# A hybrid attention trunk on one core: residual copies placed inside the paired stage, the last pair summed on chip, compression weights three pieces ahead, a shorter last norm

## The chip, the core and the metric

The kernel runs on one core of a Trainium2 chip. It computes on TensorE (PE, matmuls), VectorE (DVE), ScalarE (ACT) and GpSimd (POOL). DMA transfers are issued by the queues of SyncE (SP), POOL and, at the very start, ACT. The metric is the device time of one execution in microseconds.

## What is computed

A row of 256 tokens of width 4096 passes one layer: an RMS norm, one input projection to two mixers, a gate on each, one output projection, the residual, and a last RMS norm.

```python
h = _rmsnorm(x, norm_g[l])
proj = h @ w_in[l]
(q_a, k_a, v_a, z_a, q_b, kc, vc, ksl, vsl, kwn, vwn, z_b, g_b) = jnp.split(proj, _split_points(), axis=-1)
o_a = _dilated_mixture(...)                     # 16 heads, three strided windows
o_b = _nsa(..., kc, vc, ...)                    # 16 heads; compressed, selected and window keys
y_a = _rmsnorm(o_a, out_g_a[l]) * jax.nn.silu(z_a)
y_b = _rmsnorm(o_b, out_g_b[l]) * jax.nn.silu(z_b)
x = x + jnp.concatenate([y_a, y_b], -1) @ w_out[l]
...
return _rmsnorm(x, final_g)

# in _nsa, for the keys kc and the values vc:
def _compress(t, pe, w1, w2):                   # 15 overlapping blocks of 32 tokens
    flat = blocks(t + pe).reshape(B, n_c, G, CMP_BLOCK * hd)
    return jax.nn.gelu(flat @ w1) @ w2          # w1 is 4096 x 256, w2 256 x 128
```

All data are float32. Each product of float32 operands is done as three matmuls of operands split into a rounded high part and a remainder (`mm3`, lines 98 to 100). The high parts are written by ACT (line 105), the remainders by DVE (line 106).

## The kernel before

Weights are read from memory in chunks of 512 columns. The kernel has five stages.

1. **Start.** A stream of three single chunks. `stage_unit` loads a weight piece of 1 MB (tile `w`, line 249 to 254; three buffers), `load_xT` a piece of x transposed (tile `xp`). ACT scales and splits x (`xh`, line 108) and the weights (`wh`, line 105); DVE writes the remainders `xl` and `wl`.
2. **Paired input stage.** `run_pairs` computes nine pairs of chunks with a Strassen-like scheme: 16 steps a pair, nine of them with seven products, seven plain. Weights are loaded three steps ahead (`bw`, lines 424 and 425, on SP). The products gather in eight PSUM banks. At a pair's last product step of each kind, `put_sums` has ACT copy each bank to a tile `parts` (line 453), and POOL adds it to up to four outputs in memory with accumulating DMAs (`accum_op=add`, line 459; the first of a pair are plain stores, line 457). The ninth pair gives `sel` and `za0`.
3. **Middle stage.** A stream of eight chunks (seven gate chunks, then the first output chunk), beside which the attention work is woven in as tasks. The first tasks are the two `compress` calls (keys, then values): each reads w1 in four pieces of 1 MB (`load_w1`, line 820, SP; pool `o` with four buffers, of which the block tile `bhl` takes one), splits each piece in halves (`w1hl`) and multiplies them into `ph` (lines 872 and 873). The first two pieces are asked for ahead; piece i + 2 is asked for when piece i has been split. Each piece of the stream is called a unit; it too is split in halves.
4. **Paired output stage.** `run_pairs` again, for three pairs, with the residual added: the outputs `r1` to `r4` start as copies of columns of x (line 1326), on which `put_sums` accumulates. The last pair's sums stay on chip (`keep_first`, `keep_rest`).
5. **Last stage.** Two half chunks. ACT squares every part of the result into columns of `ssr` (`square_r`, line 1126). `finish` then sums these, takes the root on POOL (line 115), scales the rows on DVE and ACT and stores them (line 1198), first for tokens 0 to 127, then for the rest.

The paired stages stand in the order in which they are written (`manual_schedule`); in the other stages the scheduler of the language moves instructions that do not depend on what stands ahead of them. Each engine and each queue then works through its own list in order.

Of the kernel before, what the change touches and what calls it, by code (L numbers as in the profile page):

```python
# [18 lines left out]
P = 128  # L19
SEQ = 256  # L20
NT = SEQ // P
DM = 4096
# [61 lines left out]
def hybrid_trunk(ctx: ExitStack, tc: tile.TileContext, a: dict):  # L84
# [309 lines left out]

    def run_pairs(w_src, dcs, lhs_of, sops, begin, places, names, out=False, later=None):

# [76 lines left out]
        def keep_first(ps):  # L473
            t = kept["c11"] = part()
            nc.scalar.activation(t, ps["p1"], AF.Copy)
            for x, y, bank in (("c12", "c11", "p6"), ("c21", "c12", "p7"), ("c22", "c21", "p5")):
                t = kept[x] = part()
                nc.vector.tensor_add(t, kept[y], ps[bank])
            nc.vector.tensor_add(kept["c12"], kept["c12"], ps["p5"])
            for x in kept:  # L480
                nc.vector.tensor_add(kept[x], kept[x], resid[x])
# [22 lines left out]
        for n, (d, i) in enumerate(steps):  # L504
# [11 lines left out]
            if FAST[i]:  # L516
                s = lambda j: (sops[i][:, 0, j], sops[i][:, 1, j])
                e = not any(FAST[k] for _, k in steps[n + 1 : n - n % NKP + NKP])
                raws, sums = -B22, 3
                for bank, lhs, b in (  # L520
                    ("p1", block(i, 0, 0), raws + B11), ("p7", s(2), sums + T3), ("p5", s(0), sums + T1),
                    ("p6", s(1), sums + T2), ("p3", s(3), raws + B22), ("p2", block(i, 0, 1), raws + B21),
                    ("p4", block(i, 1, 1), sums + T4),
                ):
                    product(bank, lhs, b, e and bank in ("p1", "p5", "p6", "p7"))
                if e and out and d == len(dcs) - 1:
                    keep_first(ps)
                elif e:
                    put_sums(d, ps, ("p1", "p7", "p5", "p6"))
            else:  # L530
                e = n % NKP == NKP - 1
                for bank, row, cols in (("p3", 0, (B12, B22)), ("p2", 0, (B11, B21)), ("p4", 1, (B11, B21)), ("e", 1, (B12, B22))):
                    for col, b in enumerate(cols):
                        product(bank, block(i, row, col), b, e and col == 1)
                if e and d == len(dcs) - 1:
                    return lambda: keep_rest(ps) if out else put_sums(d, ps, ("p3", "p2", "p4", "e"))
                if e:
                    put_sums(d, ps, ("p3", "p2", "p4", "e"))
            split_on(n)
            if n == 2 and later:  # L540
                later()

# [286 lines left out]
    def compress(t, which):  # L829
# [26 lines left out]
        for grp in range(9):  # L856
            if grp < 8:
# [5 lines left out]
                if grp % 2 == 1:  # L863
                    load_w1(4 * which + grp // 2 + 2)
                if grp == 4 and which == 0:
# [258 lines left out]
    def square_r(pool, r, m, i):  # L1124
        junk = room[pool].tile([P, r.shape[-1]], F32, name="junk", tag="junk", bufs=1 if i == 0 else 2)
        nc.scalar.activation(junk, r, AF.Square, accum_out=ssr[:, m, i : i + 1])

# [36 lines left out]
    def out_chunk(i):  # L1164
# [3 lines left out]
        def done(ps, only=None):  # L1168
            xr, gf = res["in", i], gf_at(i)
            for m in range(NT) if only is None else [only]:  # L1170
                r = res_at(i, m)
                nc.vector.tensor_add(r, ps[m][:, : OUT_AT[i][1]], xr[:, m])
                square_r("zq", r, m, i)
                if only is None:
                    nc.vector.tensor_mul(r, r, gf)
            if only is not None:
                finish(only, gf)
        return before, done

    def finish(m, gf):  # L1180
        s = room["work"].tile([P, 1], F32, name="sr")
        nc.vector.reduce_sum(s, ssr[:, m], axis=AX.X)
        r = cst.tile([P, 1], F32, name=f"rout{m}")
        rsqrt_mean(r, s, DM)
        for i in range(8):
# [9 lines left out]
            else:  # L1195
                nc.vector.tensor_scalar_mul(t, t, r)
            if i % 2:
                nc.sync.dma_start(a["out"][m * P : (m + 1) * P, (i - 1) * CW : (i + 1) * CW],
                                  res[q, m][:, at - CW : at + CW])

# [62 lines left out]
    ordered.enter_context(tc.manual_schedule())  # L1263
    rest = run_pairs(a["w_in"], dcs, x_lhs, sops, begin_pairs, IN_PLACES, IN_BANKS)
    inner.close()
# [11 lines left out]
    def begin_rest():  # L1277
        rest()
        psum.close()
# [19 lines left out]

    hooks[0, 3] = load_first  # L1300
    hooks[0, 10] = attentions
    z_chunks = [("a", 12, i) for i in range(1, 4)] + [("b", 22, i) for i in range(4)]
# [13 lines left out]
    def before_out():  # L1316
# [7 lines left out]

        for c in range(1, 5):
            nc.gpsimd.dma_start(scratch(f"r{c}"), a["x"][:, c * CW : (c + 1) * CW].rearrange("(m p) c -> p m c", p=P))

    first_out = []
# [21 lines left out]
    ordered.enter_context(tc.manual_schedule())  # L1350
    rest = run_pairs(a["w_out"], dcs, y_lhs, y_sops, begin_out, OUT_PLACES, OUT_BANKS, out=True, later=store_first)
    inner.close()
# [76 lines left out]
```

## Time and profile before

| | us |
|---|---|
| median of three runs (lowest, highest) | 1654.27 (1653.38, 1655.62) |
| profiled execution, time | 1653.73 |
| profiled execution, span | 1651.8 |
| TensorE busy | 1615.9 |
| VectorE busy | 1377.4 |
| ScalarE busy | 999.4 |
| POOL busy | 153.6 |
| mean granted TensorE clock | 0.993 of full |

The span runs from the first to the last instruction; the time has a little around it. Matmuls overlap in the records, so a busy TensorE is not one at its peak; where it stands still is what counts. A row of a timeline gives start, duration, engine, line, operation, output tile <- input tiles, and in brackets how long the engine stood idle before it and what ended that. In rows of the chain of waits the two numbers are start and duration. The weights of `compress`, w1 and w2, read `w<-in_cmp_k_w` in the profile, since numbers at the end of a name are left out.

### The profile page before, as it was taken

To read this page: it belongs to the slowest core of one execution; us is meant where nothing else is said; L and a number is where in the kernel's file an instruction comes from. 1 tells how busy PE (TensorE), PEld (TensorE's weight loads), DVE (VectorE), ACT (ScalarE), POOL (GpSimd) and SP (SyncE) were. 2 spreads that over 40 slices of the span, in tenths; PEclk is the share of its full clock that TensorE was granted. 3 is DMA by queue.
4 is the path that set the end of the run, shared out by engine and by line. 5 is a ranking of instruction groups with operands and counts; after the bars stand their busy time and mean duration, and the time that the engine had idled before them with its cause. 6 is when DMAs were issued, how large, how long until landed. Compare 5 with 4: busy or idle time off the path is not lost.

```text
span 1651.8 us, 20933 instructions
## 1 busy us (share of the span) xinstructions
PE 1615.9 (98%) x7743; PEld 1330.4 (81%) x7743; DVE 1377.4 (83%) x1668; ACT 999.4 (61%) x1255; POOL 153.6 (9%) x207
## 2 busy tenths in 40 slices
PE   8999999999999999999998999999999999999997
PEld 5998778888888888888876777788878877788886
DVE  6769898988899898989856788888877769898884
ACT  6755656565656565656554566766667646656553
POOL 0000111110202020202020000000000000112110
PEclk9999999999999999999998999999999999999999
DMA  9776798888888887979798555633455456798974
GB/s 359 267 244 222 209 276 253 262 250 258 244 259 254 249 268 241 279 237 276 236 326 303 190 172 179 227 138 141 135 179 185 166 196 216 220 282 240 289 289 169
DMA packets 105862, 387.76 MB, mean 235 GB/s; under 512 B 12640, under 2 KB 13280, under 8 KB 94368
## 3 DMA queue, kind: packets, MB, share of 16 engines
q1 hardware_dynamic: 81504, 332.42, 57.3%
q0 software_dynamic: 23824, 52.97, 14.6%
q8 instruction: 60, 0.98, 0.2%
q10 hardware_dynamic: 432, 1.05, 0.2%
q14 instruction: 42, 0.34, 0.1%
HBM read 334.69 MB, written 53.79 MB: 235 GB/s over the span
## 4 chain that ended last, share of the span: by engine, by line
PE 81%; DVE 8%; DMA 5%; issue 3%; ACT 3%; SPq 0%; ACTq 0%; POOLq 0%; POOL 0%; DVEq 0%
PE p L99 15%; PE p L100 15%; PE p L98 15%; PE acc L99 8%; PE acc L100 8%; PE acc L98 8%; DMA w<-in_w_in 2%; PE e L100 2%; PE e L99 2%; PE e L98 2%; DVE bf L439 2%; DVE bt L432 1%; DVE bf L438 1%; DMA w<-in_cmp_k_w 1%; PE pt L1051 1%
## 5 line engine op out<-in xcount | busy, mean ns | idle before, releaser
L106 DVE TENSOR_TENSOR wl<-w,wh 128x1024 fp32r<-128x1024 f32 (+2 forms) x178 | 207.7, 1171 | 90.8 <-ACT wh L105 89.9
L105 ACT ACTIVATE wh<-w 128x1024 fp32r<-128x1024 f32 (+2 forms) x178 | 180.3, 1017 | 111.5 <-PE acc L100 92.4
L98 PE MATMUL acc<-wh,xh 128*128 128x512 f32 (+2 forms) x640 | 244.3, 382 | 3.3 <-ACT wh L105 3.2
L439 DVE TENSOR_TENSOR bf<-bt,bf 128x2048 fp32r<-128x2048 f32 x108 | 246.6, 2283 | 0.0
L99 PE MATMUL acc<-wl,xh 128*128 128x512 f32 (+2 forms) x640 | 241.7, 378 | 2.8 <-DVE wl L106 2.8
L100 PE MATMUL acc<-wh,xl 128*128 128x512 f32 (+2 forms) x640 | 241.3, 377 | 0.0
L434 ACT ACTIVATE bf<-bt 128x1024 fp32r<-128x1024 f32 x108 | 114.6, 1061 | 185.6 <-DVE bt L432 185.3
L106 DVE TENSOR_TENSOR bp<-bw,bp 128x2048 fp32r<-128x2048 f32 x72 | 164.7, 2287 | 72.5 <-ACT bp L105 72.4
L431 ACT ACTIVATE bf<-bw 128x1536 fp32r<-128x1536 f32 x108 | 160.5, 1486 | 65.9 <-DMA bw<-in_w_in 42.6
L105 ACT ACTIVATE bp<-bw 128x2048 fp32r<-128x2048 f32 x72 | 137.7, 1912 | 92.3 <-PE e L100 73.8
L438 DVE TENSOR_TENSOR bf<-bw,bf 128x1536 fp32r<-128x1536 f32 x108 | 189.0, 1750 | 0.0
L437 ACT ACTIVATE bf<-bt 128x1024 fp32r<-128x1024 f32 x108 | 114.8, 1063 | 42.8 <-DVE bt L436 40.2
L432 DVE TENSOR_TENSOR bt<-bw 128x1024 f32<-128x1024 f32 x108 | 131.8, 1221 | 10.0 <-DMA bw<-in_w_in 5.5
L98 PEld LDWEIGHTS acc<-wh,xh 128*128 128x128 f32 x640 | 121.3, 190 | 22.2 <-ACT wh L105 5.4
L99 PEld LDWEIGHTS acc<-wl,xh 128*128 128x128 f32 x640 | 121.4, 190 | 22.0 <-DVE wl L106 5.8
L100 PEld LDWEIGHTS acc<-wh,xl 128*128 128x128 f32 x640 | 121.1, 189 | 19.0
L99 PE MATMUL p<-bf,sum 128*128 128x512 f32 x324 | 127.0, 392 | 1.4 <-DVE bf L439 1.2
L99 PE MATMUL p<-bp,xh 128*128 128x512 f32 x324 | 126.2, 389 | 0.9 <-DVE bp L106 0.9
L98 PE MATMUL p<-bf,sum 128*128 128x512 f32 x324 | 126.3, 390 | 0.0
L100 PE MATMUL p<-bf,sum 128*128 128x512 f32 x324 | 126.2, 390 | 0.0
L100 PE MATMUL p<-bp,xl 128*128 128x512 f32 x324 | 126.0, 389 | 0.0
L98 PE MATMUL p<-bp,xh 128*128 128x512 f32 x324 | 126.0, 389 | 0.0
(325 smaller groups left out, 3413.0 us busy)
## 6 DMA issues: line engine op xcount, KB each, us to landing
bw<-in_w_in SPq DMA_DIRECT2D x288, 512.0 KB, 6.3
w<-in_w_in SPq DMA_DIRECT2D x60, 1024.0 KB, 5.0
bw<-in_w_out SPq DMA_DIRECT2D x96, 512.0 KB, 5.1
w<-in_w_out SPq DMA_DIRECT2D x16, 1024.0 KB, 5.1
scr_q<-parts POOLq DMA_DIRECT2D x30, 256.0 KB, 7.9
scr_k<-parts POOLq DMA_DIRECT2D x30, 256.0 KB, 7.9
scr_v<-parts POOLq DMA_DIRECT2D x30, 256.0 KB, 7.8
scr_qb<-parts POOLq DMA_DIRECT2D x30, 256.0 KB, 7.9
```

The lines of the kernel that those rows point to most:

```text
L98: nc.tensor.matmul(out, lh, rh, start=start, stop=False)
L99: nc.tensor.matmul(out, lh, rl, start=False, stop=False)
L100: nc.tensor.matmul(out, ll, rh, start=False, stop=stop)
L105: nc.scalar.activation(h, src, AF.Copy)
L106: nc.vector.tensor_sub(l, src, h.bitcast(F32))
L431: nc.scalar.activation(h[:, :3], w[:, B22:], AF.Copy)
L432: nc.vector.tensor_tensor(t[:, T3 : T1 + 1], w[:, B22 : B11 + 1], w[:, B12 : B12 + 1].to_broadcast([P, 2, CW]), op=OP.subtract)
L434: nc.scalar.activation(h[:, 3:5], t[:, T3 : T1 + 1], AF.Copy)
L437: nc.scalar.activation(h[:, 5:], t[:, T2:], AF.Copy)
L438: nc.vector.tensor_sub(l[:, :3], w[:, B22:], h[:, :3].bitcast(F32))
L439: nc.vector.tensor_sub(l[:, 3:], t, h[:, 3:].bitcast(F32))
L1051: nc.tensor.transpose(pt[:rows, j], src, ident)
```

## The change

Four edits in one:

- The four copies of x to `r1` to `r4` are issued inside the paired input stage, after steps 24, 48, 72 and 96, and not in `before_out`.
- The ninth pair of the input stage keeps its sums on chip as the last output pair did (`keep_first`, `keep_rest`: DVE adds), and POOL stores the four blocks once each.
- `compress` asks for piece i + 3; piece 2 is asked for ahead by a hook of the middle stage.
- In `finish`, the squares of the last half chunk are summed by DVE in one instruction and not by ACT; the sum over the other parts is made ahead of it; the first two of 512 columns are stored singly.

```diff
@@ run_pairs, keep_first
-            for x in kept:
+            for x in resid:
                 nc.vector.tensor_add(kept[x], kept[x], resid[x])
...
-                if e and out and d == len(dcs) - 1:
+                if e and d == len(dcs) - 1:
                     keep_first(ps)
...
-                    return lambda: keep_rest(ps) if out else put_sums(d, ps, ("p3", "p2", "p4", "e"))
+                    return lambda: keep_rest(ps)
...
-            if n == 2 and later:
-                later()
+            if n in later:
+                later[n]()
@@ compress
-                    load_w1(4 * which + grp // 2 + 2)
+                    load_w1(4 * which + grp // 2 + 3)
@@ square_r
-        nc.scalar.activation(junk, r, AF.Square, accum_out=ssr[:, m, i : i + 1])
+        nc.scalar.activation(junk, r, AF.Square, scale=DM ** -0.5, accum_out=ssr[:, m, i : i + 1])
@@ out_chunk, the last half chunk
+                    mean = room["work"].tile([P, 1], F32, name="mean")
+                    nc.vector.reduce_sum(mean, ssr[:, m, :i], axis=AX.X)
+                    nc.vector.tensor_scalar_add(mean, mean, EPS)
+                    nc.vector.tensor_add(r, ps[m][:, : OUT_AT[i][1]], xr[:, m])
+                    finish(m, r, gf, mean)
@@ finish
-        nc.vector.reduce_sum(s, ssr[:, m], axis=AX.X)
+        nc.vector.scalar_tensor_tensor(junk, last, 1.0 / DM, last, op0=OP.mult, op1=OP.mult, accum_out=ss)
+        nc.vector.tensor_add(t, ss, mean)
-        rsqrt_mean(r, s, DM)
+        nc.gpsimd.tensor_tensor(r, t, nhalf[:, :1], op=OP.pow)
...
-            if i % 2:
-                nc.sync.dma_start(a["out"][m * P : (m + 1) * P, (i - 1) * CW : (i + 1) * CW],
-                                  res[q, m][:, at - CW : at + CW])
+            cols = {0: (0, 1), 1: (1, 2), 3: (2, 4), 5: (4, 6), 7: (6, 8)}.get(i)
+            if cols:
+                c0, c1 = cols[0] * CW, cols[1] * CW
+                nc.sync.dma_start(a["out"][m * P : (m + 1) * P, c0:c1], ...)
@@ the program
+    def put_residual(c):
+        nc.gpsimd.dma_start(scratch(f"r{c}"), a["x"][:, c * CW : (c + 1) * CW].rearrange("(m p) c -> p m c", p=P))
+    residuals = {24 * c: (lambda c=c: put_residual(c)) for c in range(1, 5)}
+    rest = run_pairs(a["w_in"], dcs, x_lhs, sops, begin_pairs, IN_PLACES, IN_BANKS, later=residuals)
...
     def begin_rest():
-        rest()
+        for x, t in rest().items():
+            m, c = int(x[1]) - 1, int(x[2]) - 1
+            nc.gpsimd.dma_start(scratch(("sel", "za0")[c])[:, m], t)
...
+    hooks[0, 8] = lambda: load_w1(2)
... in before_out:
-        for c in range(1, 5):
-            nc.gpsimd.dma_start(scratch(f"r{c}"), a["x"][:, c * CW : (c + 1) * CW].rearrange("(m p) c -> p m c", p=P))
```

What this does to the order is not all in the diff. **POOL, the head of its list, before.** The copies to `scr_r` depend on nothing, so the scheduler had put them ahead of everything else, at the start of the kernel:

```order
L1418 MEMSET const-uint8-127 128x1
L1425 UNCONDITIONAL_BRANCH
L1326 DMA scr_r_10346<-in_x 256x1x512
L1326 DMA scr_r_10348<-in_x 256x1x512
L1326 DMA scr_r_10350<-in_x 256x1x512
L1326 DMA scr_r_10352<-in_x 256x1x512
L115 ISA
L115 TENSOR_TENSOR rstd<-rsq,nhalf 128x2
```

POOL at the end of the first pair, now:

```order
L459 DMA scr_q_1645<-parts 128x512
L459 DMA scr_q_1646<-parts 128x512 x2
L459 DMA scr_q_1645<-parts 128x512 x2
L459 DMA scr_q_1646<-parts 128x512
L1277 DMA scr_r_1986<-in_x 256x1x512
L457 DMA scr_k_2121<-parts 128x512
L457 DMA scr_k_2122<-parts 128x512
```

The first copy stands between the first pair's last accumulation and the second pair's first store; the other three stand likewise behind the third, fourth and sixth pair.

**SP, the beginning of the middle stage, before.** The rows from `in_cmp_k_w` are pieces of w1 (128x2048), those from `in_w_in` units of the stream:

```order
L820 DMA w_5842<-in_cmp_k_w 128x2048
L820 DMA w_5844<-in_cmp_k_w 128x2048
L254 DMA w<-in_w_in 128x2048 x3
L824 DMA pe<-in_cmp_v_pe 128x32
L560 DMA fetched<-scr_v_2627 128x1024
L826 DMA w_6011<-in_cmp_v_w 128x256
L254 DMA w<-in_w_in 128x2048
L820 DMA w_5950<-in_cmp_k_w 128x2048
L820 DMA w_5990<-in_cmp_k_w 128x2048
L820 DMA w_6036<-in_cmp_v_w 128x2048
```

The same place now:

```order
L820 DMA w_5836<-in_cmp_k_w 128x2048
L820 DMA w_5838<-in_cmp_k_w 128x2048
L254 DMA w<-in_w_in 128x2048 x2
L820 DMA w_5886<-in_cmp_k_w 128x2048
L254 DMA w<-in_w_in 128x2048
L824 DMA pe<-in_cmp_v_pe 128x32
L560 DMA fetched<-scr_v_2629 128x1024
L826 DMA w_6007<-in_cmp_v_w 128x256
L254 DMA w<-in_w_in 128x2048
L820 DMA w_5946<-in_cmp_k_w 128x2048
L254 DMA w<-in_w_in 128x2048
```

The third piece has moved ahead of two units and three small loads; the fourth piece stands where the third was, one unit ahead of the value weights.

**ACT, the same stage, one piece of the difference.** `wh` are halves of stream units, `w1hl` halves of w1's first piece, `parts` the evictions of the ninth pair:

```order
 L105 ACTIVATE wh<-w 128x1024 x3
-L453 ACTIVATE parts<-p_1200 128x512
-L453 ACTIVATE parts<-p_1196 128x512
-L453 ACTIVATE parts<-p_1197 128x512
-L453 ACTIVATE parts<-e 128x512
-L105 ACTIVATE w2h<-w_5840 128x256
-L105 ACTIVATE wh<-w 128x1024
-L105 ACTIVATE w1hl<-w_5842 128x1024 x2
-L105 ACTIVATE wh<-w 128x1024 x4
+L105 ACTIVATE w2h<-w_5834 128x256
+L105 ACTIVATE w1hl<-w_5836 128x1024 x2
+L105 ACTIVATE wh<-w 128x1024 x5
```

Seven evictions are gone from ACT in all (three more stand above this piece), and the fourth half of the stream now comes behind both halves of w1's first piece, where it came ahead of them. TensorE's own order is the same in both kernels.

More of the change, by code (lines that the diff above doesn't have):

```diff
@@ L393, in hybrid_trunk, with run_pairs @@
     OUT_PLACES, OUT_BANKS = ("f1", "t", "p", "f0", "w"), ("p7", "p1", "p6", "p5", "p4", "p2", "p3", "e")
-    def run_pairs(w_src, dcs, lhs_of, sops, begin, places, names, out=False, later=None):
+    def run_pairs(w_src, dcs, lhs_of, sops, begin, places, names, out=False, later={}):
         fast, plain = [[i for i in range(NKP) if FAST[i] == f] for f in (1, 0)]
@@ L1171, in done, with finish @@
                 r = res_at(i, m)
-                nc.vector.tensor_add(r, ps[m][:, : OUT_AT[i][1]], xr[:, m])
-                square_r("zq", r, m, i)
                 if only is None:
+                    nc.vector.tensor_add(r, ps[m][:, : OUT_AT[i][1]], xr[:, m])
+                    square_r("zq", r, m, i)
                     nc.vector.tensor_mul(r, r, gf)
-            if only is not None:
-                finish(only, gf)
-        return before, done
-    def finish(m, gf):
-        s = room["work"].tile([P, 1], F32, name="sr")
-        nc.vector.reduce_sum(s, ssr[:, m], axis=AX.X)
+                else:
+                    mean = room["work"].tile([P, 1], F32, name="mean")
+                    nc.vector.reduce_sum(mean, ssr[:, m, :i], axis=AX.X)
+                    nc.vector.tensor_scalar_add(mean, mean, EPS)
+                    nc.vector.tensor_add(r, ps[m][:, : OUT_AT[i][1]], xr[:, m])
+                    finish(m, r, gf, mean)
+        return before, done
+    def finish(m, last, gf, mean):
+        junk = room["zq"].tile([P, last.shape[-1]], F32, name="junk", tag="junk", bufs=2)
+        ss = room["work"].tile([P, 1], F32, name="sr")
+        nc.vector.scalar_tensor_tensor(junk, last, 1.0 / DM, last, op0=OP.mult, op1=OP.mult, accum_out=ss)
+        t = room["work"].tile([P, 1], F32, name="rsq")
+        nc.vector.tensor_add(t, ss, mean)
         r = cst.tile([P, 1], F32, name=f"rout{m}")
-        rsqrt_mean(r, s, DM)
+        nc.gpsimd.tensor_tensor(r, t, nhalf[:, :1], op=OP.pow)
         for i in range(8):
@@ L1196, in finish @@
                 nc.vector.tensor_scalar_mul(t, t, r)
-            if i % 2:
-                nc.sync.dma_start(a["out"][m * P : (m + 1) * P, (i - 1) * CW : (i + 1) * CW],
-                                  res[q, m][:, at - CW : at + CW])
+            cols = {0: (0, 1), 1: (1, 2), 3: (2, 4), 5: (4, 6), 7: (6, 8)}.get(i)
+            if cols:
+                c0, c1 = cols[0] * CW, cols[1] * CW
+                nc.sync.dma_start(a["out"][m * P : (m + 1) * P, c0:c1],
+                                  res[q, m][:, c0 - q * DM // 2 : c1 - q * DM // 2])
     def w_chunk(col):
@@ L1263, in hybrid_trunk @@
     ordered.enter_context(tc.manual_schedule())
-    rest = run_pairs(a["w_in"], dcs, x_lhs, sops, begin_pairs, IN_PLACES, IN_BANKS)
+    def put_residual(c):
+        nc.gpsimd.dma_start(scratch(f"r{c}"), a["x"][:, c * CW : (c + 1) * CW].rearrange("(m p) c -> p m c", p=P))
+    residuals = {24 * c: (lambda c=c: put_residual(c)) for c in range(1, 5)}
+    rest = run_pairs(a["w_in"], dcs, x_lhs, sops, begin_pairs, IN_PLACES, IN_BANKS, later=residuals)
     inner.close()
@@ L1350, in hybrid_trunk @@
     ordered.enter_context(tc.manual_schedule())
-    rest = run_pairs(a["w_out"], dcs, y_lhs, y_sops, begin_out, OUT_PLACES, OUT_BANKS, out=True, later=store_first)
+    rest = run_pairs(a["w_out"], dcs, y_lhs, y_sops, begin_out, OUT_PLACES, OUT_BANKS, out=True, later={2: store_first})
     inner.close()
```

## The prediction

> **What bounds the kernel now.** I read the busy shares first, then busy time by stretches, then the chain and DMA queues where TensorE falls short. Of each stretch: length, busy time (instructions) of each engine, granted TensorE clock, DMA share, GB/s.
>
> ```profile
> span 1651.8 us, 20933 instructions
> PE 1615.9 (98%) x7743; PEld 1330.4 (81%) x7743; DVE 1377.4 (83%) x1668; ACT 999.4 (61%) x1255; POOL 153.6 (9%) x207
> ...
> 6.20:15.88 9.68, 7.13 (x25) 4.20 (x24) 5.32 (x10) 4.92 (x10) 0.66 (x1) 1.00 1.03 414
> 15.88:25.00 9.12, 7.23 (x23) 5.56 (x24) 7.19 (x11) 8.01 (x14) 0.00 (x0) 0.81 1.03 418
> 843.00:872.90 29.90, 27.85 (x135) 21.71 (x133) 16.24 (x15) 12.81 (x14) 7.42 (x10) 1.00 1.08 329
> 872.90:878.70 5.80, 0.04 (x1) 0.05 (x1) 0.06 (x1) 1.15 (x2) 0.00 (x0) 0.75 1.05 362
> 878.70:890.00 11.30, 10.51 (x46) 8.88 (x47) 7.63 (x7) 6.25 (x7) 0.00 (x0) 0.68 0.83 328
> 700.00:725.00 25.00, 25.00 (x112) 20.69 (x111) 24.73 (x19) 14.94 (x12) 3.46 (x4) 1.00 0.91 282
> ```
>
> TensorE bounds the kernel: full in the paired stage (last row), short only at the seams. So time is to be had where TensorE stands still or runs at a low clock: at the start, and after 843 us. In both places the DMA share is above 1, and the chain names transfers there (start, duration):
>
> ```profile
> 5.69 10.19 DMA w<-in_w_in
> 15.90 1.06 ACT wh L105
> 16.99 1.24 DVE wl L106
> 861.73 15.72 DMA w<-in_cmp_k_w
> ```
>
> What fills the queues: first the stretch 0 to 15.9 us, then 836 to 878 us (packets, MB, share of the 16 engines' time; q0 holds POOL's transfers).
>
> ```profile
> q0 software_dynamic: 514, 1.91, 29.7%
> scr_r<-in_x POOLq DMA_DIRECT2D x4, 512.0 KB, 9.2
> ...
> q1 hardware_dynamic: 2101, 10.18, 64.2%
> q0 software_dynamic: 1587, 2.89, 37.4%
> cmat<-in_consts SPq DMA_DIRECT2D x1, 784.0 KB, 4.5
> ```
>
> In the first, the only transfers on q0 are the four residual copies, written in the code as part of the output chunk but standing first on POOL. They hold 0.297 x 15.9 = 4.7 us of all engines' time ahead of the weight piece on which the chain waits. In the second, q0 is the accumulating stores of the last pair: 0.374 x 42 = 15.7 us for 2.89 MB, 5.4 us per MB against 0.642 x 42 / 10.18 = 2.65 for loads.
>
> **Part 1, the residual copies leave the start.** The order puts each behind a pair's last accumulation. Bandwidth alone brings the waited piece forward 4.7 us, to 11.2. ScalarE, which splits x and weights, then has to follow:
>
> ```profile
> 10.74 0.51 ACT L108 ACTIVATE xh<-xp,g_in 128x256 fp32r<-128x256 f32 x1 [1.03 <-DMA xp<-in_xT]
> 11.16 0.61 ACT L105 ACTIVATE wh<-w 128x512 fp32r<-128x512 f32 x1
> 12.72 0.91 ACT L108 ACTIVATE xh<-xp,g_in 128x256 fp32r<-128x256 f32 x2
> 17.01 0.49 PE L98 MATMUL acc<-wh,xh 128*128 128x512 f32 x1 [1.62 <-ACT wh L105]
> 18.27 0.50 PE L99 MATMUL acc<-wl,xh 128*128 128x512 f32 x1 [0.77 <-DVE wl L106]
> ```
>
> The third x slice waited for its load until 10.74. At the stretch's mean share the copies held 0.297 x 10.74 = 3.2 us by then; ScalarE, which needs 1.12 us a slice, can use about 1.8 of it, so that slice starts near 8.9. Two slices at 0.51 + 0.61, two more x splits 0.91, the weight split 1.06: 8.9 + 2.24 + 0.91 + 1.06 = 13.1, and VectorE's 1.24 brings the second product to 14.3 against 18.27: 4.0 us. The clock row 15.88 to 25 adds 9.12 x 0.19 = 1.7 us lost to the dip after this stall. The remaining gaps (about 0.3 and 0.8 us) are half of today's, so I count 1.0 of it: 5.0 in all. Bounds: 2.0 (the piece still late by half) and 4.7 + 1.7 = 6.4. Nothing eats it later before 180 us: after 25 us TensorE is fed and waited for.
>
> The Trainium skill, "TensorE: Matmul & The Clock Gate", Part 1, says the clock falls to half after an idle window of about 3.4 us. Here it fell after gaps of 1.62 and 0.77 us, so page and trace differ and the measurement decides. By the page's rule alone gaps this short would not dip, the whole 1.7 us would return, and the sum below would be 0.7 us better.
>
> In the paired stage each copy adds 4.72 / 1.91 x 0.52 = 1.3 us of the engines' time, behind the accumulations. Cover: weights three steps ahead, TensorE full, VectorE at most 24.73 of 25 us. If VectorE cannot catch up, TensorE loses up to 1.3 four times, 5.2 us. I take 0.3. On POOL nobody queues behind a copy for long:
>
> ```profile
> 225.98 0.86 POOL L459 DMA_DIRECT2D scr_q<-parts  x1 [1.76 <-issue]
> 263.59 2.19 POOL L457 DMA_DIRECT2D scr_k<-parts  x4 [36.75 <-ACT parts L453]
> ```
>
> POOL waits 36.75 us there; an issue takes under 1 us.
>
> **Part 2, the last pair and compression.** These rows are the ones that end TensorE's waits after 843 us, and the engines ahead of them:
>
> ```profile
> 847.95 0.42 ACT L105 ACTIVATE w2h<-w 128x256 fp32r<-128x256 f32 x1 [5.14 <-DMA w<-in_cmp_k_w]
> 850.49 2.01 ACT L105 ACTIVATE w1hl<-w 128x1024 fp32r<-128x1024 f32 x2 [1.18 <-DMA w<-in_cmp_k_w]
> 850.63 0.50 PE L99 MATMUL acc<-wl,xh 128*128 128x512 f32 x1
> 855.14 0.50 PE L99 MATMUL acc<-wl,xh 128*128 128x512 f32 x1 [1.14 <-DVE wl L106]
> 866.66 2.01 ACT L105 ACTIVATE w1hl<-w 128x1024 fp32r<-128x1024 f32 x2 [1.49 <-PE ph L873]
> 878.66 0.47 PE L872 MATMUL ph<-w1hl,bhl 128*60 128x256 f32 x1 [5.79 <-ACT w1hl L105]
> ```
>
> The third weight piece is asked for at 861.73 and lands at 877.45. Now SP asks for it two w loads earlier, and instead of 15.7 us of accumulating traffic there are four plain stores (1.05 MB x 2.65 = 2.8 us), so 12.9 us of engine time come free of the 42. Asked for near 851 it lands near 860, while ScalarE can use it only from 866.66 + 2.01 = 868.7: no wait. The fourth, behind one more w load, has until about 871. So the 5.76 us stall goes, and with it the clock loss behind it, 11.30 x 0.32 = 3.6 us: 9.4.
>
> The rest of the idle time from 843 to 890 is 2.05 + 0.79 = 2.84 us. There ScalarE's order changes against us: both halves of w1's first piece now stand ahead of a weight half that TensorE uses at 850.63. That piece is asked for behind cmat, the compression input (0.52 MB) and w2 (0.13 MB); with its own 1.05 MB that is 2.5 x 2.65 = 6.6 us from about 836.8, when this batch starts, plus the landing lag of cmat (4.5 - 0.80 x 2.65 = 2.4): 845.8, or 848.6 if all four stores cut in. Then 2.01 + 1.06 on ScalarE and 1.23 on VectorE: 850.1 to 852.9, so a wait of 0 to 2.3 us, against which today's 1.14 us at 855.14 falls away. I count 0.6 of the 2.84 as gained: 10.0 for the part. Bounds: 9.4 + 2.84 = 12.2, and 6.4 (none of the 2.84 gained, 2.3 - 1.14 = 1.2 added, half the dip kept: 9.4 - 1.2 - 1.8).
>
> The sums move from ScalarE to VectorE: eight adds, seven evictions less.
>
> ```profile
> L485 DVE TENSOR_TENSOR parts<-parts,p x3: 678/679/679, 1592.5 to 1593.7; 128x512 f32<-128x512 f32 x3
> ...
> 833.21 3.50 DVE L106 TENSOR_TENSOR wl<-w,wh 128x1024 fp32r<-128x1024 f32 x3 [0.20 <-ACT wh L105]
> 842.21 0.60 ACT L453 ACTIVATE parts<-e 128x512 f32<-128x512 f32 x1 [0.76 <-PE e L100]
> ```
>
> Four stand ahead of the first three weight halves (done at 836.7 today, then 836.7 + 4 x 0.68 = 839.4; TensorE comes to them after the pair's last product, 842.2). The other four end near 843; the next VectorE work then waits for a transfer until about 843 anyway. The stores read on POOL behind two memsets; what they write is fetched after 1019 us. Cost 0; without that cover 2.7 us.
>
> **Part 3, the last norm.** The chain after the last matmul:
>
> ```profile
> 1641.63 0.42 ACT L1126 ACTIVATE junk<-r 128x256 f32<-128x256 f32 x1 [7.57 <-DVE r L1172]
> 1642.37 0.15 DVE L114 TENSOR_SCALAR rsq<-sr 128x1 f32<-128x1 f32 x1
> 1642.60 0.55 POOL L115 TENSOR_TENSOR rout<-rsq,nhalf 128x1 f32<-128x1 f32 x1 [10.93 <-DVE rsq L114]
> 1643.19 1.67 DVE L1196 TENSOR_SCALAR r<-r,rout 128x512 f32<-128x512 f32 x4 [0.67 <-POOL rout L115]
> 1643.94 2.88 SPq L1198 DMA_DIRECT2D out<-r  x4
> L666 DVE SCALAR_TENSOR_TENSOR n<-n,cmat x32: 283/355/426, 941.4 to 1043.6; 128x128 f32<-128x128 f32 x16, 128x256 f32<-128x256 f32 x16
> L666 DVE DVE_READ_ACCUMULATOR n<-n,cmat x32: 80/83/86, 941.6 to 1044.0; 128x1 f32 x32
> ```
>
> From ScalarE's square at 1641.63 to POOL at 1642.60 is 0.97 us. New, on VectorE: square and sum 0.43 + 0.08, one small add 0.15, two handovers of about 0.06: 0.78, and one handover ahead of the square less: 0.24 saved; the sum of the earlier chunks is done before TensorE ends. The first store leaves after one scaling (0.42) instead of 0.75: 0.33 more. Stores then run to the end without a break, so both count: 0.6. Bounds 0 (the last piece decides) and 0.9.
>
> **Sum.** 5.0 - 0.3 + 10.0 + 0.6 = 15.3 us. The profiled execution took 1653.73 (span 1651.8 and 1.9 around it), 0.54 under the median 1654.27 of three runs from 1653.38 to 1655.62. 1653.73 - 15.3 = 1638.4; against the median, 1639.0.
>
> **Rivals.** (a) The start is paced by issue and splits, not by bandwidth: 2.0 instead of 5.0, 1642.0. For it: ScalarE's rows above leave little room; against: its waits name transfers. (b) The wait moves to the weight half behind w1: 6.4 instead of 10.0, 1642.6; with the dip left whole, 1644.4. (c) The load of the third piece is early but the stage stays choked, since 8 MB of compression weights remain: the stall halves and the dip stays, 10.0 becomes 3, 1646. Against: 12.9 of 42 us freed. (d) The other side: the copies starve the paired stage. VectorE at 24.73 of 25 speaks for it; but to lose the whole gain and 0.2% each copy must cost TensorE (15.3 + 3.3) / 4 = 4.6 us, 3.6 times what it holds the engines; at its bound of 5.2 - 0.3 the time is 1643.9, and past 4.6 each it is 1657.6 or more. (e) All bounds at their best: 6.4 + 12.2 + 0.9, 1634.8.
>
> **How the numbers follow.** Forecast 0.62 (1636 to 1641.5), (a) 0.12, (b) 0.12, (c) 0.06, (d) 0.02, (e) 0.03, and 0.03 that gains cancel. The range reaches to (e) and nearly to (c): 1634.5 to 1645.5. A measurement here tells about 0.2%, 3.3 us, from no change. Faster: all but (d) and the cancelling: 0.95; same 0.03; slower 0.02.
>
> **What would show it.** Right: no q0 packets in the first 16 us, and TensorE's second weight unit near 14 us; q0 under 8% from 836 to 878; no wait over 2 us on w1hl, clock 1.00 there; 25.00 busy around 226, 388, 467 and 630 us; first last-norm store about 2.4 us after the last matmul. Wrong: w1hl still named by a transfer, a wait of over 2 us at the weight half behind it, or TensorE under 24 of 25 us behind a copy.

## The result and the profile after

The changed kernel takes 1636.35 us, the median of four runs (1634.81 to 1638.11), against 1654.94 us of the kernel before in the same session: ratio 0.9889, 95% interval 0.9872 to 0.9906. Forecast were 1639.0 us and the range 1634.5 to 1645.5; the gain is 18.6 us by these medians and 18.4 between the profiled executions, where 15.3 were summed up. The profiled execution took 1635.38 us, with a span of 1633.6.

Its page, busy time and instructions of each engine:

```profile
span 1633.6 us, 20920 instructions
PE 1608.6 (98%) x7743; PEld 1327.4 (81%) x7743; DVE 1383.3 (85%) x1682; ACT 994.7 (61%) x1244; POOL 142.8 (9%) x196
```

TensorE does the same 7743 matmuls in 7.3 us less busy time: they are not fewer, but some took longer before. The dips of the clock in the rows below were worth 1.7 us at the start (9.12 x 0.19) and 3.6 in the middle (11.30 x 0.32) of that. The stretches that bounded the kernel before, in the same columns (length, busy time of PE, PEld, DVE, ACT, POOL, clock, DMA share, GB/s):

```profile
6.20:15.88 9.68, 8.14 (x31) 5.79 (x32) 8.00 (x14) 8.27 (x17) 0.00 (x0) 1.00 1.03 405
15.88:25.00 9.12, 9.12 (x40) 7.35 (x39) 8.98 (x17) 7.95 (x15) 0.00 (x0) 1.00 1.03 417
843.00:872.90 29.90, 29.32 (x161) 24.21 (x159) 23.02 (x20) 18.51 (x20) 0.00 (x0) 1.00 0.94 361
872.90:890.00 17.10, 17.10 (x87) 13.76 (x86) 14.21 (x24) 10.22 (x16) 0.00 (x0) 1.00 0.84 321
```

TensorE is full where it stood at 7.23 of 9.12 us and at 0.04 of 5.80, and the clock rows of 0.81, 0.75 and 0.68 have become 1.00. The DMA share of the start is still 1.03: the engines are as busy as before, with other transfers. The queues from 0 to 15.9 us, then the two that matter from 828 to 878 us:

```profile
q1 hardware_dynamic: 1638, 3.91, 63.5%
q10 hardware_dynamic: 432, 1.05, 21.4%
...
q1 hardware_dynamic: 2880, 15.78, 82.2%
q0 software_dynamic: 320, 1.05, 5.2%
```

No q0 in the start, and 5.2% of it in the middle. Where the gains lie is read from marks that both traces have: the same instruction of the chain of waits at the first seam of the paired stage, the load of `cmat`, the end of the keys' compression (`halves`), the last matmul, and the end of the span. Rows of before, then of after (before, this instruction of the chain stood at 179.63):

```profile
L1285 SPq DMA_DIRECT2D cmat<-in_consts x1: 328/328/328, 836.8 to 836.8; - x1
L876 ACT ACTIVATE halves<-ph x2: 361/362/362, 890.8 to 919.7; 60x256 f32<-60x256 f32 x2
1640.79 0.28 PE L100 MATMUL acc<-eh,yl 128*128 128x256 f32 x1
```

```profile
174.31 1.93 ACT bp L105
L1303 SPq DMA_DIRECT2D cmat<-in_consts x1: 327/327/327, 830.9 to 830.9; - x1
L876 ACT ACTIVATE halves<-ph x2: 362/362/362, 872.9 to 901.9; 60x256 f32<-60x256 f32 x2
1623.21 0.28 PE L100 MATMUL acc<-eh,yl 128*128 128x256 f32 x1
```

The lead is 5.3 us at the seam, 5.9 at `cmat` (nothing lost in the paired stage), 17.9 at the end of the keys (so 12.0 in the middle), 17.6 at the last matmul, and 18.2 at the end of the span (so 0.6 in the last norm).

### The profile page after: what moved, and what is told of

Same layout as the page of the kernel before. It is cut to its first block, busy times and chain, and to the rows that moved or that the text cites. A ratio compares the mean times of both kernels' runs of the same rounds, so it can differ in the third digit from the quotient of the medians.

```text
span 1633.6 us, 20920 instructions
## 1 busy us (share of the span) xinstructions
PE 1608.6 (98%) x7743; PEld 1327.4 (81%) x7743; DVE 1383.3 (85%) x1682; ACT 994.7 (61%) x1244; POOL 142.8 (9%) x196
## 4 chain that ended last, share of the span: by engine, by line
PE 89%; DVE 5%; issue 2%; ACT 2%; DMA 2%; SPq 0%; ACTq 0%; POOLq 0%; POOL 0%
PE p L99 16%; PE p L100 16%; PE p L98 16%; PE acc L99 9%; PE acc L100 9%; PE acc L98 9%; PE e L100 2%; PE e L99 2%; PE e L98 2%; DVE bf L439 1%; PE pt L1051 1%; DVE bt L432 1%; PE pt L597 1%; DVE bf L438 1%; ACT bp L105 1%
```

## The experiments

Two questions were open: what in the start and in the middle had been the cause, since three edits act on the middle at once, and whether the four parts are independent of one another. In the middle, the theories were: T1, the accumulating stores held the DMA engines; T2, the third piece of w1 was asked for too late; T3, both are needed; later T4, ScalarE's shorter list brought the gain.

**Each part alone, on the kernel before.**

> The kernel before with one edit alone: the four residual copies are issued inside the paired stage. Bandwidth theory (the copies held the transfers of the start back): TensorE's second weight unit starts near 14 us and not at 15.88 to 18.27, the granted clock stays 1.00 in 15 to 25 us, the first seam of the paired stage (row 'ACT bp L105' of the chain) lies 5.0 to 5.5 us earlier than at 179.6, and it stays that much earlier up to the load of the compression input at 836.8; time 5.0 to 5.5 us less (about 1649). Rival (a copy in the paired stage costs TensorE something behind each accumulation): the lead shrinks by over 1 us between 180 and 836, TensorE under 24.9 of 25 us in a stretch that holds a copy. Rival (the start is paced by issue and splits): the seam gains 2 us or less. The middle stage is as before: 5.8 us of stall at w1hl and the dip of the clock behind it stay.

> The kernel before with one edit alone: the ninth pair's sums are made on chip and stored once. Theory T1 (the 15.7 us of engine time of the accumulating stores choked the loads of the middle stage; when the third piece of w1 is asked for is of no account): the whole 12 us of the middle come, the wait on w1hl falls under 0.5 us, clock 1.00; time about 1642. Rival T2 (the third piece was asked for too late, behind units whose buffers came free late): the piece is still asked for only near 857, lands near 863 to 866, and ScalarE has waited for it: 6 to 8 us gained, a wait of 1 to 3 us on w1hl stays. Rival T3 (both are needed): 3 to 6 us gained, the clock still dips below 0.9 between 865 and 890. The start is as before.

> The kernel before with one edit alone: w1 is asked for three pieces ahead; the ninth pair still accumulates in memory, so q0 still holds the engines for 15.7 us. T1: with the queues as full as before, an earlier request for the third piece delays the stream units that now stand behind it by as much (2.7 us a piece): 0 to 3 us gained in the middle, TensorE idle between 843 and 890 still over 5 us in sum, clock under 0.9 in part of it. T2: the wait of 5.8 us on w1hl goes and with it the dip: 7 to 10 us gained. T3: 3 to 6 us gained. Start and last norm as before.

> The kernel before with one edit alone: the shorter chain of the last norm. The prediction's sum: 0.24 us of chain and 0.33 us of the first store, so the time from the last matmul's end to the end of the span falls by 0.6 us (bounds 0 to 0.9), the first store leaves about 2.4 us after the last matmul and not 2.87. Rival (the last stored piece decides, and all stores move 1 MB at the same rate): the first store leaves earlier, the span ends at the same distance from the last matmul, 0 us. The median of the runs cannot tell 0.6 us; the trace's rows do.

The edits are the pieces of the diff above, one at a time: `residuals`/`put_residual`; `keep_first`, `keep_rest` and the four stores in `begin_rest`; `grp // 2 + 3` with the hook `load_w1(2)`; `square_r` and `finish`.

| | median us | ratio to before (95%) | seam at | `cmat` to end of keys |
|---|---|---|---|---|
| before | 1654.79 | | 179.63 | 54.0 |
| copies alone | 1647.51 | 0.9957 (0.9945 to 0.9970) | 173.76 | 53.9 |
| sums on chip alone | 1642.63 | 0.9925 (0.9911 to 0.9938) | 179.26 | 43.3 |
| three ahead alone | 1651.34 | 0.9982 (0.9973 to 0.9991) | 180.31 | 49.7 |
| last norm alone | 1653.66 | 0.9994 (0.9984 to 1.0004) | 180.81 | 54.2 |
| all four (before in its session: 1654.94) | 1636.35 | 0.9889 (0.9872 to 0.9906) | 174.31 | 42.0 |

The stretch from the load of `cmat` to the end of the keys, one row each: before, then sums on chip, three ahead, and all four.

```profile
836.80:890.80 54.00, 45.40 (x214) 36.53 (x213) 24.63 (x22) 23.40 (x27) 10.06 (x13) 0.91 0.99 323
```

```profile
835.70:879.00 43.30, 41.68 (x214) 34.17 (x214) 29.53 (x29) 21.11 (x23) 2.61 (x6) 1.00 0.95 345
```

```profile
838.80:888.50 49.70, 43.25 (x219) 34.93 (x217) 24.06 (x22) 23.04 (x27) 9.94 (x13) 1.00 1.03 335
```

```profile
830.90:872.90 42.00, 41.42 (x214) 34.22 (x212) 29.59 (x29) 21.30 (x23) 2.61 (x6) 1.00 0.94 357
```

The sums on chip alone bring 10.7 of the 12.0 us, the early request alone 4.3, and the two are not additive. T2's reading of the request is right (with the sums on chip alone the third piece is asked for at 858.48, and ScalarE waits 2.92 us for it, where T1 had expected under 0.5), but the price is small: 1.3 us. T2 falls: it had 7 to 10 us for the early request. T3 had 3 to 6 us for each edit alone; the 4.3 of the early request lie in that range, the 10.7 of the sums on chip do not, so T3 falls too. T1 holds in the main, though its "no more than 3" for the early request is missed by 1.3. What the early request cannot do is seen in ScalarE's rows of that kernel:

```profile
877.98 1.05 ACT L105 ACTIVATE wh<-w 128x1024 fp32r<-128x1024 f32 x1
886.56 1.06 ACT L105 ACTIVATE w1hl<-w 128x1024 fp32r<-128x1024 f32 x1 [6.59 <-DMA w<-in_cmp_v_w]
```

The wait has left the keys' third piece and gone to the values' first, 6.59 us; TensorE stands for 4.47 us ahead of 888.88. With the queues as full as before, the earlier place of one piece was a later one for another.

The copies alone bring the seam forward by 5.9 us, a little more than the 5.0 to 5.5 expected, and the whole lead is still there at 830.7 (`cmat`); the rivals (issue pace, 2 us or less; a cost behind each accumulation) fall. By the medians 7.3 us are gained, with an interval of 5.0 to 9.1. Over all kernels of this study the seam stands at 179.3 to 180.8 with the four copies at the start and at 173.6 to 174.3 without them, so 6 us are the better figure. The last norm alone is within the noise of the runs, as expected; from the last matmul (1643.79) to the end of the span (1654.2) are 10.4 us, against 11.0 before (1640.79 to 1651.8).

**Is it the traffic?** The changed kernel, with the stores put back as spare work:

```diff
+        def spare(after, blocks):
+            z = part()
+            nc.gpsimd.memset(z, 0.0)
+            nc.vector.tensor_copy(z[:, :1], after[:, :1])
+            for b in blocks:
+                nc.gpsimd.dma_start(scratch(f"spare{b // 2}")[:, b % 2], z, accum_op=OP.add)  # second run: without accum_op
@@ keep_first   + spare(kept["c22"], (2, 3, 1, 3, 1, 2, 3))
@@ keep_rest    + spare(kept["c22"], (1, 0, 2, 3))
```

> The changed kernel, with accumulating stores put back as spare work: eleven stores of 256 KB with an accumulation, from tiles of zeros onto memory that nobody reads, seven behind the last product of seven and four behind the end of the ninth pair, issued by POOL (four plain stores of zeros to the same memory go ahead of them in an earlier pair, under a full TensorE). ScalarE keeps its shorter list, VectorE its adds, w1 stays three pieces ahead. T1 (the traffic of the accumulating stores was the cause): q0 rises from 1.05 MB and 5% to about 4 MB and over 30% between 828 and 878 us, and most of what the on-chip sums brought in company of the early request (12.0 - 4.3 = 7.7 us) is lost again: from the load of the compression input to the end of the keys 42.0 becomes 47 to 50 us, time 1641 to 1645. Rival T4 (the gain came from ScalarE, rid of seven evictions, and from its new order): under 2 us are lost, time 1636 to 1638.

> As the run above with eleven spare stores, but plain ones without an accumulation (and none in the earlier pair). If an accumulation costs the engines twice the time of a plain store (5.4 us a MB against 2.6 to 2.8), q0 shows about 4 MB at 18 to 22% between 828 and 878 us, and the loss is half or less of that of the accumulating ones: 42.0 becomes 43 to 46 us. Rival (an accumulation costs no more than its bytes; what chokes is the number of stores): the same share and the same loss as with the accumulating ones.

The queue q0 and the stretch from `cmat` to the end of the keys, with accumulating stores, with plain ones, and q0 of the changed kernel:

```profile
q0 software_dynamic: 1904, 3.93, 36.7%
830.70:886.40 55.70, 44.89 (x218) 36.26 (x217) 29.19 (x30) 20.92 (x22) 12.02 (x18) 0.91 1.00 321
```

```profile
q0 software_dynamic: 1200, 3.93, 21.2%
833.80:882.70 48.90, 44.46 (x213) 36.25 (x213) 29.58 (x30) 21.17 (x22) 8.39 (x17) 0.93 0.97 365
```

```profile
q0 software_dynamic: 320, 1.05, 6.1%
```

The stretch takes 55.7 and 48.9 us where the changed kernel takes 42.0 (in all 1649.08 us, ratio 0.9968, 0.9957 to 0.9979, and 1645.23 us, 0.9949, 0.9929 to 0.9969). But not all of this loss is the traffic's: the spare code adds a wait of its own. Its small copy on VectorE waits for a memset on POOL, which stands behind spare stores that wait for each other, and VectorE's remainders stand behind that copy. With accumulating stores, then with plain ones:

```profile
850.65 0.15 DVE L476 COPY parts<-parts 128x1 f32<-128x1 f32 x1 [7.76 <-POOL parts L475]
```

```profile
848.69 0.15 DVE L476 COPY parts<-parts 128x1 f32<-128x1 f32 x1 [4.40 <-POOL parts L475]
```

In the changed kernel VectorE starts on w1's first half 1.1 us behind ScalarE (841.72 and 840.63). By that distance it would start at 845.6 and 847.5 in these two runs (ScalarE at 844.46 and 846.42); it starts at 850.73 and 848.77. So, as an estimate, 5.2 of the 13.7 us and 1.3 of the 6.9 are the spare code's. At most 8.5 and 5.6 us are left to the stores: the clock dips behind the wait (0.91 and 0.93 in the rows above), and part of that may be the spare code's too. Without the spare code's share the stretch is 50.5 and 47.6 us, so the expected 47 to 50 and 43 to 46 were a little too small. T4 falls even so. With the whole rise of TensorE's busy time (44.89 - 41.42 = 3.5) taken off, 5.0 us remain, where T4 had under 2; and ScalarE gets w1's first piece 3.8 us later than in the changed kernel (844.46 and 840.63), though `cmat` is asked for at the same time (830.7 and 830.9).

What a us of the engines' time costs TensorE in this stage is therefore only bounded. q0's engine time is 20.4 us with accumulating stores (0.367 x 55.7), 10.4 with plain ones and 2.6 in the changed kernel, so at most 0.5 us per us (8.5 of 17.8) and 0.7 (5.6 of 7.8). From before to the sums on chip q0's time falls by 13.1 (0.291 x 54.0 = 15.7 to 2.6) and 10.7 come back, 0.8 per us, with ScalarE's seven evictions gone as well. The engines' own price does not hang on the waits: an accumulation costs (20.4 - 2.6) / 2.88 MB = 6.2 us per MB, a plain store 10.4 / 3.93 = 2.6, so the rival of equal shares falls.

The place of the new waits is the one that the prediction's rival (b) named, the weight half behind w1. With accumulating stores:

```profile
847.46 0.50 PE L98 MATMUL acc<-wh,xh 128*128 128x512 f32 x1 [3.19 <-ACT wh L105]
854.28 0.80 PE L99 MATMUL acc<-wl,xh 128*128 128x512 f32 x1 [6.32 <-DVE wl L106]
```

Without the 5.2 us of the spare code this is 4.3 us, against 0.58 in the changed kernel with free queues. The old order under full queues (the copies alone) had 0.40, 0.55 and 1.14 us at the weight halves there. No run changes ScalarE's order alone.

**Do copies cost nothing in the paired stage?** Four copies at each place and not one:

```diff
-        nc.gpsimd.dma_start(scratch(f"r{c}"), a["x"][...])
+        for key in (f"r{c}", f"x{c}", f"y{c}", f"z{c}"):
+            nc.gpsimd.dma_start(scratch(key), a["x"][...])
```

> The changed kernel with four copies of 0.5 MB at each of the four places in the paired stage, one to the residual and three to memory that nobody reads. The engines are held 4 x 1.3 = 5.2 us a place. The prediction's cover (weights three steps ahead, 16% of the engines' time free on average): TensorE still 25.00 of 25 us around 225, 385, 465 and 628 us, time within 1 us of the changed kernel's. Rival (d, the copies starve the paired stage; the bound of the prediction was 1.3 us lost for each 1.3 us held): up to 15.6 us more are lost, TensorE under 24 of 25 us there, and a wait for DMA bw is named.

The 16 us from each place's first copy on:

```profile
221.00:237.00 16.00, 16.00 (x71) 12.95 (x70) 15.79 (x13) 9.65 (x9) 2.71 (x4) 1.00 1.04 374
381.00:397.00 16.00, 16.00 (x73) 13.24 (x72) 15.40 (x12) 9.20 (x8) 2.69 (x4) 1.00 1.03 377
459.00:475.00 16.00, 16.00 (x73) 13.24 (x72) 15.83 (x12) 8.57 (x8) 2.69 (x4) 1.00 1.04 360
624.00:640.00 16.00, 16.00 (x72) 13.28 (x71) 15.83 (x13) 9.73 (x8) 2.70 (x4) 1.00 1.04 367
```

The engines are full (share 1.03 to 1.04, where the changed kernel has 0.85 to 0.92) and TensorE loses nothing: 1635.30 us, ratio 0.9892 (0.9876 to 0.9907). Rival (d) is out. That the loads three steps ahead carry it is the prediction's reading; no run changes their number. Single traces of other kernels show a gap of TensorE of 0.6 to 1.2 us here and there in this stage, with copies in it (ahead of 479.87 in the run with plain spare stores) and without (ahead of 484.17 with the last norm alone), so a loss of that size in some executions is not excluded.

**Is the start a matter of bandwidth?** The kernel before, with two copies moved and two left: `residuals = {24 * c: ... for c in (3, 4)}`, and `put_residual(c)` for 1 and 2 in `before_out`.

> The kernel before with two of the four residual copies moved into the paired stage and two left at the head of POOL's list. All four moved brought the first seam of the paired stage from 179.6 (179.3 to 180.8 over the kernels that left the start alone) to 173.8 us. Bandwidth theory (what counts is the time for which the copies hold the engines, 1.2 us each): about half, the seam at 176 to 178 us, clock between 0.85 and 1.00 in 15 to 25 us. Rival 1 (any copy ahead of the loads delays the first pieces): the seam stays after 178.5. Rival 2 (only the overload counts, two copies fit in): the seam comes before 175.

```profile
q0 software_dynamic: 288, 1.05, 16.4%
176.37 1.93 ACT bp L105
7.00:13.00 6.00, 5.30 (x15) 3.76 (x16) 4.03 (x8) 3.93 (x9) 0.00 (x0) 0.72 1.03 413
```

With half the bytes at the start the seam stands at 176.4, 3.6 of the 6 us gained (1651.04 us, 0.9977, 0.9968 to 0.9987): half the copies are worth about half, as the bandwidth theory has it. The clock was a miss: it is 1.00 in 15 to 25 us, and dips earlier, in 7 to 13 us, for as much.

**A version that beats both.** Among what is left in the changed kernel are waits of TensorE for VectorE behind the seams: 2.1 us between 175 and 225, 4.1 us between 1325 and 1450. A first try halved a few splits (`for b in ((0, 2), (2, 4)) if n in halved`):

> A version that should beat both: the changed kernel, with the splits of a few steps of the paired stages done in two halves, so that TensorE need not wait for the whole of 2.3 us. In the first input pair's successor steps 17 and 19, in the output stage steps 6, 17 and 19. In the profile of the changed kernel TensorE waits there for VectorE: 0.85 us at 190.3, 1.24 at 203.4, 1.23 at 1342.2, 0.89 at 1358.5, 0.69 at 1414.7, 1.24 at 1427.8 us. An instruction on half the columns ends 1.05 us sooner and costs about 0.2 us more in all; where ScalarE's part is halved too VectorE starts 0.9 us sooner. Theory: the four gaps at 17 and 19 and the one at step 6 go, 4 to 5 us, time about 1631.5 to 1632.5. Rival (VectorE's throughput sets the end of the streak and not the last instruction's length): the gaps come back at the next step, 0 to 1.5 us gained.

1635.26 us, 0.9887 (0.9872 to 0.9902): the rival was right. The gap at 203.4 went and one of 1.12 us came at 217.85. So VectorE's order was changed for the whole run of steps:

```diff
-                nc.vector.tensor_sub(l[:, :3], w[:, B22:], h[:, :3].bitcast(F32))
-                nc.vector.tensor_sub(l[:, 3:], t, h[:, 3:].bitcast(F32))
+                    low = lambda at, src: nc.vector.tensor_sub(l[:, at], src, h[:, at].bitcast(F32))
+                    low(slice(1, 2), w[:, B11 : B11 + 1])
+                    low(slice(3, 5), t[:, T3 : T1 + 1])
+                    low(slice(5, 7), t[:, T2:])
+                    low(slice(0, 3, 2), w[:, B22 : B21 + 1 : 2])
...
+        halved = range(2 if out else 17, 33)        # second version: N for 33
```

> The changed kernel, with VectorE's remainders of steps 17 to 32 (input pairs) and 2 to 32 (output pairs) written in the order in which TensorE asks for them: block B11, sums T3 and T1, sums T2 and T4, then B22 and B21 in one instruction; plain steps in two halves on ScalarE and VectorE. In the version with a few halves the gap came back one or two steps later (1.12 us at 217.9, 0.94 at 1372.5, 0.95 at 1441.0), since VectorE is behind for a whole run of steps. Theory: the wait at the end of such a run is the distance between VectorE's start on a step's remainders and the first sum's being ready; it falls from 4.0 us (1.75 + 2.28) to 1.8 us (0.61 + 1.22), which is more than any of the gaps, so the 2.1 us between 175 and 225 and the 4.1 us between 1325 and 1450 go but for 1 us: 4 to 5 us faster than the changed kernel, about 1631. Rival (throughput alone: four instructions in place of two cost 0.15 us more a step): the gaps move on again, within 1 us of the changed kernel.

> As the run above, but in every later step of the paired stages too. Those steps show no gap in the changed kernel (600.00 of 600 us between 225 and 825), so on the theory nothing more is to be had: the same time within 0.5 us. Rival: 0.15 us more on VectorE a step take its slack where it is busy 24.7 of 25 us, and gaps of 0.2 us or more appear at the steps between 225 and 825: 1 to 3 us slower than the run above.

> The version with VectorE's remainders in TensorE's order at all later steps, timed once more, since the first interval of its ratio (0.9845 to 0.9878) still touches that of the changed kernel (0.9872 to 0.9906). Theory: the gain of 4 to 5 us over the changed kernel is there again, ratio 0.985 to 0.987; TensorE 24.9 of 25 us or more in 200 to 225 us and 124 of 125 between 1325 and 1450. Rival (the first timing was a lucky chip): ratio 0.988 to 0.989, as the changed kernel.

The first version took 1633.13 us (0.9870, 0.9849 to 0.9890), the second 1630.62 (0.9861, 0.9845 to 0.9878) and again 1631.56 (0.9862, 0.9845 to 0.9879). The two stretches behind the seams, the changed kernel and the second version's two profiles:

```profile
175.00:225.00 50.00, 47.91 (x206) 37.95 (x205) 45.31 (x34) 31.80 (x30) 12.60 (x16) 1.00 0.91 252
1325.00:1450.00 125.00, 120.91 (x518) 96.22 (x517) 117.19 (x88) 73.17 (x66) 13.50 (x16) 1.00 0.74 221
```

```profile
175.00:225.00 50.00, 49.91 (x217) 40.01 (x216) 45.52 (x45) 31.85 (x33) 12.62 (x16) 1.00 0.90 243
1325.00:1450.00 125.00, 124.21 (x537) 99.93 (x536) 121.76 (x129) 75.88 (x75) 13.52 (x16) 1.00 0.77 232
```

```profile
175.00:225.00 50.00, 48.53 (x210) 38.52 (x209) 43.60 (x42) 30.14 (x32) 12.63 (x16) 1.00 0.91 242
212.89 1.23 DVE L433 TENSOR_TENSOR bt<-bw 128x1024 f32<-128x1024 f32 x1 [1.64 <-DMA bw<-in_w_in]
```

In the output stage 3.3 of 4.1 us come back in both. In the input stage 2.0 or 0.6 of 2.1 come back in the stretch shown, but a gap stands just behind it in both profiles, as it does in that of the first version (0.87 us ahead of 232.31):

```profile
231.03 0.50 PE L99 MATMUL p<-bf,xh 128*128 128x512 f32 x1 [0.60 <-DVE bf L440]
```

```profile
233.07 0.50 PE L99 MATMUL p<-bf,xh 128*128 128x512 f32 x1 [0.85 <-DVE bf L440]
```

From 175 to 825 us TensorE stands still for 0.9 and 2.5 us (first version 2.5), against 2.1 in the changed kernel. So in the input stage the rival was right in two traces of three: the gaps moved on. VectorE, no longer behind, waits there for the weights' load itself (up to 1.64 us). The gain is in the output stage: from `cmat` to the last matmul the two profiles take 787.4 and 788.1 us, the changed kernel 792.3.

By the medians the second version is 5.7 and 4.8 us below the changed kernel. The intervals of their ratios overlap by less than 0.001, and the two were not timed in one session; the second timing and the two other kernels that run as the changed one does (0.9892, 0.9887) speak for the difference. That the later steps help by themselves is not shown: the two versions' intervals overlap widely.

## Why the prediction held, point by point

- **Bound and places.** Right: both gains lie where TensorE stood still or ran at a low clock with the DMA share above 1, and the rest of the program kept its length (from the keys to the last matmul 750.0 before, 750.3 after).
- **Start, 5.0 (2.0 to 6.4).** Right in mechanism, a little low: 5.3 in this pair of traces, 5.9 with the copies alone. The weight half of unit 1 was to bring the second product to 14.3; its remainder is done at 14.25 (start and duration):

```profile
13.02 1.23 DVE L106 TENSOR_TENSOR wl<-w,wh 128x1024 fp32r<-128x1024 f32 x1
```

  The second product follows at 14.49, 3.8 us earlier than before (forecast 4.0). The mis-sized piece is the dip of the clock: I kept 0.7 of its 1.7 us for gaps of 0.3 and 0.8 that would remain, but TensorE has no gap after 10.17 us and the clock is 1.00 from 6.20 to 25 us. By the rule of the Trainium skill, "TensorE: Matmul & The Clock Gate", Part 1 (a dip follows an idle window of about 3.4 us), the start would be 5.7, between the 5.3 and the 5.9 measured. The rule isn't borne out by that, since the gaps themselves went.
- **Copies in the paired stage, 0.3 lost.** Nothing was lost in this pair of traces, and not even four times the copies cost anything in theirs. The bound of 5.2 was far too wide: I had named the cover, three steps of loads ahead, and not priced it. Between the first copy (221.6) and the last (624.2) lie 72 steps, 5.6 us each, so three steps are 17 us, against 1.3 us of engine time a copy and 5.2 us for four.
- **Middle, 10.0 (6.4 to 12.2).** This is the term that was mis-sized: 12.0. Idle time fell from 8.60 (54.00 - 45.40) to 0.58 us, so 8.0 and not 5.76 + 0.6; the busy time fell by the other 4.0 (45.40 - 41.42), where I had 3.6 for the clock. The step that failed is "0.6 of the 2.84 counted as gained". The wait at the weight half behind w1 is there and in its range (0 to 2.3 us), at 0.58; but I left the other short gaps standing without looking at what ended each. In the kernel with the copies alone, whose middle is that of before, they read:

```profile
844.92 0.50 PE L99 MATMUL acc<-wl,xh 128*128 128x512 f32 x1 [0.40 <-DVE wl L106]
848.31 0.49 PE L98 MATMUL acc<-wh,xh 128*128 128x512 f32 x1 [0.55 <-ACT wh L105]
849.95 0.50 PE L99 MATMUL acc<-wl,xh 128*128 128x512 f32 x1 [1.14 <-DVE wl L106]
860.12 0.33 PE L872 MATMUL ph<-w1hl,bhl 128*60 128x256 f32 x1 [0.56 <-DVE bhl L106]
874.55 0.47 PE L873 MATMUL ph<-w1hl,bhl 128*60 128x256 f32 x1 [0.79 <-DVE w1hl L106]
```

  All of these are gone in the changed kernel; that the splits waited because their pieces came late is my reading of it. One gap is left (last row; ScalarE's rows ahead of it):

```profile
840.63 2.01 ACT L105 ACTIVATE w1hl<-w 128x1024 fp32r<-128x1024 f32 x2 [2.07 <-DMA w<-in_cmp_k_w]
842.54 3.01 ACT L105 ACTIVATE wh<-w 128x1024 fp32r<-128x1024 f32 x3
845.27 0.50 PE L99 MATMUL acc<-wl,xh 128*128 128x512 f32 x1 [0.58 <-DVE wl L106]
```

  ScalarE's 2.07 us there are over the 2 us that I had named as a sign of failure, but it had nothing else to do and TensorE was fed. The sum also let the earlier request and the freed engines end the 5.76 us stall together; the freed engines alone do nearly all of it (10.7 of the 12.0 us).
- **Last norm, 0.6.** Right: 11.0 to 10.4 us, and the first store leaves 2.30 us after the last matmul's end (forecast 2.4):

```profile
1625.79 3.01 SPq L1208 DMA_DIRECT2D out<-r  x5
```

- **Rivals.** (a), (c) and (d) did not occur. (b) appears at its place when the traffic is put back, with 4.3 us after the spare code's share. (e), all bounds at their best, gave 1634.8 and is nearer to the measured 1636.35 than the forecast's 1639.0: start, copies and middle all came out on the good side. In the start and the middle one thing was overlooked twice, that a freed queue ends the small gaps and the dip together with the large wait.

## What to carry to other kernels

Where the DMA share is at 1 and a wait names a transfer, ask first what else holds the engines in that stretch, in engine time and not in bytes: here 2.9 MB of accumulating stores held them for 15.7 us, and taking these out was worth 10.7 us, while asking earlier for the late piece alone was worth 4.3 and moved the wait to the next piece. Traffic that nobody waits for belongs where loads run several steps ahead; here even full engines (share 1.03 to 1.04) cost nothing there. Where one engine is behind for a run of steps, shortening one instruction moved the gap on; putting its work in the order of its reader brought back 3.3 of 4.1 us in the output stage, but little in the input stage, where the loads were the next limit. And work put back to test a cause can wait by itself: its own instructions have to be looked for in the trace before the loss is put down to the cause.

## What was not expected of the hardware

- A store with an accumulation cost 6.2 us of the 16 engines' time per MB, a plain one to the same memory 2.6, by the queue's share in the rows above; in the kernel before, the accumulating stores of the last pair cost 5.4 (15.7 us for 2.88 MB). So the accumulating one was 2.1 to 2.4 times as dear.
- The dip of the clock at the start cost the same in two kernels: 1.7 us in the kernel before (9.12 x 0.19) and 1.7 us with two copies left (6.00 x 0.28); behind the longer stall of the middle it cost 3.6 (11.30 x 0.32). At the start it followed gaps that were not much longer than some that it did not follow: 1.83 us ahead of 7.70 with two copies left, with a dip, and 1.60 us ahead of 7.21 in the changed kernel, without one (second row):

```profile
7.70 0.98 PE L98 MATMUL acc<-wh,xh 128*128 128x512 f32 x2 [1.83 <-ACT wh L105]
```

```profile
7.21 0.73 PE L98 MATMUL acc<-wh,xh 128*128 128x512 f32 x2 [1.60 <-ACT wh L105]
```

  The Trainium skill, "TensorE: Matmul & The Clock Gate", Part 1, describes windows of about 3.4 us that run freely and are not started by the kernel. Half the clock over one such window is 1.7 us, an estimate from the page's figure that agrees with the two dips at the start, and a dip that depends on where in a window a gap falls is in keeping with these rows. That the window must be idle as a whole is not: 1.83 us is about half of one, and the 1.62 and 0.77 us of the kernel before together 0.7 of one. Which share of a window is enough no run here shows.
